# Prompt attention by pairs of heads, side by side on halves of TensorE's rows and columns

## The chip, the core and the metric

The kernel runs on one core of a Trainium2 chip. The core has TensorE (PE), VectorE (DVE), ScalarE (ACT), GpSimd (POOL) and SyncE (SP), each with its own instruction stream, kept in step by semaphores. Operands lie in SBUF; TensorE writes to PSUM, and VectorE, ScalarE or GpSimd carry results from there to SBUF. The metric is the device time in microseconds, lower is better.

## The reference

The program is one inference step of a decoder trunk of two layers, width 1024, for 256 new prompt tokens and 8 sequences of 8 sample tokens with 1024 past tokens each. A layer projects the tokens, mixes them by three head groups side by side (a Mamba-2 scan "SSD", causal pooling, and sparse attention "NSA"), adds an output projection, and ends with a convolutional feed-forward network. The change is in the prompt's part of the attention, which is, for four heads of width 64 and blocks of 128 queries:

```python
qb_len = min(Q_BLOCK, t)                                    # Q_BLOCK = 128, t = 256
def query_block(args):
    qb, gb, s = args
    sc = jnp.einsum('bqhd,bnd->bhqn', qb, ck)               # compressed keys
    pc = masked_softmax(sc, (cmp_end[None, :] <= tpos[:, None])[None, None])
    o_cmp = jnp.einsum('bhqn,bnd->bqhd', pc, cv)
...
    ss = jnp.einsum('bqhd,bqsd->bhqs', qb, kg)              # selected blocks
    ps = masked_softmax(ss, smask[:, None])
    o_slc = jnp.einsum('bhqs,bqsd->bqhd', ps, vg)
...
    sw = jnp.einsum('bqhd,bkd->bhqk', qb, kw)               # window
    pw = masked_softmax(sw, wmask[None, None])
    o_win = jnp.einsum('bhqk,bkd->bqhd', pw, vw)
    return gb[..., 0:1] * o_cmp + gb[..., 1:2] * o_slc + gb[..., 2:3] * o_win
```

All heads share one set of keys and values. With 256 prompt tokens there are four blocks of 64 to select from and 16 may be selected, so every block is taken.

## The kernel before

All 320 tokens (256 prompt, 64 sample) go through the dense products together. A dense product is a tile `mt` in PSUM: 128 outputs by 320 tokens, to which three products of split numbers are added (`xh` by `wh`, `xl` by `wh`, `xh` by `wl`). ScalarE makes the high part `wh` of a weight tile and VectorE the low part `wl`. Products of the attention are in plain fp32, and TensorE takes each of them in two passes.

A layer is cut into steps that a string names, one string for each layer. Those that matter here are `pr` (nsa_prep: turns queries and keys so that the head width of 64 lies on the partitions), `p0` and `p1` (prompt_scores for the first and second block of queries), `o0` and `o1` (prompt_out), `n0` and `n1` (new_rows: turned rows of the sample tokens in a tile `kn`), `s0` and `s1` (sample_scores of the two groups of four sequences), `l0` and `l1` (sample_load), `g` and `r0`, `r1` (gathers and the rest of the sample's attention), `st`, `c0` to `c3`, `x`, `z` (steps of the SSD). The numbers behind `@` are priorities. The tile framework's list scheduler puts the instructions of all steps in one order for each engine, by readiness and priority, and the pieces of `mt` are what it fills TensorE with. A table `ENG` says for some copies which engine makes them.

nsa_prep leaves the keys in `KT` (64 partitions: 256 keys of the selected kind, 16 compressed ones, 256 of the window) and the queries in `qT`, one slice of 64 partitions for each head. prompt_scores makes, for each head and key range (0 to 271, and for the second block also 272 to 527), one product `sc` into a PSUM tile, which VectorE or ScalarE carries to `Sx` (and VectorE the compressed keys' part to `Cx`); then maxima, exponentials, sums, and the weights scaled in place. prompt_out turns the compressed weights (`pct`) and, head by head, the others (`pT` in PSUM, `PT` in SBUF), and adds the products with the values to a tile `O` of two halves of 64 partitions, one for each head of a pair. Inside prompt_out, TensorE's instructions keep the order in which they are written. The PSUM pool `ns`, from which `sc`, `pT`, `O`, `kn`, `sC` and `sD` come, has three buffers.

SyncE issues the DMAs in its own order. A gather of cached rows (`cache<-cslc`) is 16 DMAs, each behind a load of a page number into a register. `wk` (line 1027) is the load of a sample group's window keys and values; `h<-s_ssm` loads the SSD states of the sample sequences.

## Time and profile before

| | before |
|---|---|
| median of 3 runs | 1232.06 us (1231.94 to 1237.4) |
| profiled execution | 1224.47 us |
| its span | 1222.3 us |
| granted TensorE clock, mean | 0.97 of full speed |
| busy: PE / DVE / ACT / POOL | 96% / 66% / 44% / 25% |
| DMA | 180.18 MB, 147 GB/s over the span |

The span is the time from the first to the last instruction of the one execution that the profiler recorded; that execution was 7.6 us faster than the median. A share of busy time is a mean over the whole span, so stretches are read apart from each other.

### The profile page before, as it was taken

How to read it: one execution, taken by the hardware profiler on the slowest of the kernel's cores; microseconds unless marked ns; L12 is line 12 of the kernel's file. 1: busy time of each engine (PE TensorE's matmuls, PEld its weight loads, DVE VectorE, ACT ScalarE, POOL GpSimd, SP SyncE). 2: the span in 40 equal slices, each digit the busy share in tenths (PEclk: the TensorE clock that was granted, in tenths of full speed). 3: DMA queues.
4: the chain of work that ended last, by engine and by line, in shares of the span. 5: the costliest groups of instructions: out<-in, count | busy, mean ns of one | idle time of the engine just before them, and what ended most of it. 6: DMA issues, size and time to landing. Idle time of an engine off the chain costs nothing.

```text
span 1222.3 us, 23199 instructions
## 1 busy us (share of the span) xinstructions
PE 1171.7 (96%) x8450; PEld 1093.2 (89%) x8450; DVE 802.5 (66%) x1661; ACT 536.7 (44%) x950; POOL 302.5 (25%) x616
## 2 busy tenths in 40 slices
PE   7999998899999999999999999889999999999995
PEld 6799765599999999999999877778899999999995
DVE  4583667368756666656663688986685666666665
ACT  5445523236454444433433565433455444444431
POOL 4732222100513113311300033440342311111111
PEclk9999999699999999999999999898899999999998
DMA  7634227355555455545433445206345544445421
GB/s 277 191 100 137 76 85 252 100 161 185 175 177 199 167 168 181 159 146 184 156 104 105 154 131 189 99 27 199 119 138 171 165 143 159 152 145 158 150 72 43
DMA packets 85186, 180.18 MB, mean 147 GB/s; under 512 B 10449, under 2 KB 45009, under 8 KB 84049
## 3 DMA queue, kind: packets, MB, share of 16 engines
q1 hardware_dynamic: 84048, 176.61, 45.0%
q0 software_dynamic: 1024, 2.10, 0.6%
q8 instruction: 66, 1.08, 0.4%
q14 instruction: 48, 0.39, 0.1%
HBM read 168.97 MB, written 13.83 MB: 150 GB/s over the span
## 4 chain that ended last, share of the span: by engine, by line
PE 88%; DVE 5%; POOL 2%; ACT 2%; issue 1%; DMA 1%; SPq 1%; DVEq 0%; POOLq 0%; ACTq 0%
PE mt L283 67%; PE cs L283 5%; PE nat L283 4%; PE sn L283 1%; PE O L283 1%; PE sb L283 1%; PE sc L283 1%; PE yoh L283 1%; PE ss L283 1%; PE pe L283 1%; PE rb L283 1%; PE pT L287 1%; DMA h<-s_ssm 1%; PE sA L283 1%; DVE xt L437 1%
## 5 line engine op out<-in xcount | busy, mean ns | idle before, releaser
L342 ACT ACTIVATE wh<-raw 128x1024 fp32r<-128x1024 f32 (+2 forms) x156 | 159.9, 1026 | 199.7 <-PE mt L283 147.2
L283 PE MATMUL mt<-xh,wa 128*128 128x320 f32 x1024 | 237.2, 310 | 0.0
L283 PE MATMUL mt<-xl,wh 128*128 128x320 f32 x736 | 232.0, 315 | 0.0
L283 PE MATMUL mt<-xh,wl 128*128 128x320 f32 x736 | 231.2, 314 | 0.0
L283 PE MATMUL mt<-xh,wh 128*128 128x320 f32 x736 | 230.9, 315 | 0.2 <-ACT xh L421 0.2
L290 DVE TENSOR_TENSOR wl<-raw,wh 128x1024 fp32r<-128x1024 f32 (+2 forms) x151 | 179.5, 1189 | 68.2 <-ACT wh L342 65.5
L283 PEld LDWEIGHTS mt<-xh,wa 128*128 128x128 f32 x1024 | 174.8, 188 | 0.3
L283 PE MATMUL mt<-xl,wa 128*128 128x320 f32 x512 | 158.5, 310 | 0.0
L283 PEld LDWEIGHTS mt<-xh,wh 128*128 128x128 f32 x736 | 138.9, 189 | 5.8 <-issue 5.0
L283 PEld LDWEIGHTS mt<-xh,wl 128*128 128x128 f32 x736 | 138.8, 189 | 4.6 <-issue 3.9
L283 PEld LDWEIGHTS mt<-xl,wh 128*128 128x128 f32 x736 | 139.0, 189 | 3.2 <-issue 2.4
L290 DVE TENSOR_TENSOR wa<-raw,wa 128x1024 fp32r<-128x1024 f32 x92 | 113.5, 1234 | 37.2 <-ACT wa L342 36.9
L290 POOL TENSOR_TENSOR fa<-fa,fc 128x256 f32<-128x256 f32 (+1 forms) x128 | 82.0, 662 | 191.5 <-ACT fc L1171 136.8
L342 ACT ACTIVATE wa<-raw 128x1024 fp32r<-128x1024 f32 x92 | 96.8, 1053 | 48.4 <-DMA raw<-wg 34.9
L283 PE MATMUL mt<-act,wa 128*128 128x320 f32 x768 | 117.8, 309 | 0.0
L283 PEld LDWEIGHTS mt<-act,wa 128*128 128x128 f32 x768 | 114.0, 188 | 0.0
L283 PE MATMUL mt<-act,wh 128*128 128x320 f32 x512 | 113.2, 309 | 0.0
L283 PEld LDWEIGHTS mt<-xl,wa 128*128 128x128 f32 x512 | 96.3, 188 | 0.0
L1164 POOL COPY off<-fext 128x2 f32<-128x2 f32 x64 | 19.5, 304 | 283.2 <-DVE fext L290 283.2
L283 PEld LDWEIGHTS mt<-act,wh 128*128 128x128 f32 x512 | 85.6, 188 | 0.0
L290 DVE TENSOR_TENSOR fo<-fo,mt 128x320 f32<-128x320 f32 x112 | 54.0, 484 | 44.6 <-PE mt L283 44.3
L283 PE MATMUL mt<-act,wl 128*128 128x320 f32 x256 | 79.1, 309 | 0.0
(375 smaller groups left out, 1976.2 us busy)
## 6 DMA issues: line engine op xcount, KB each, us to landing
raw<-wg SPq DMA_DIRECT2D x168, 512.0 KB
raw<-wd SPq DMA_DIRECT2D x64, 512.0 KB
cache<-cslc SPq DMA_DIRECT2D x128, 64.0 KB
cache<-ccmp SPq DMA_DIRECT2D x96, 64.0 KB
w<-w SPq DMA_DIRECT2D x4, 1024.0 KB
o_sss<-h SPq DMA_DIRECT2D x16, 256.0 KB
o_winold<-wnat SPq DMA_DIRECT2D x16, 252.0 KB
raw<-wnb SPq DMA_DIRECT2D x8, 384.0 KB
```

The costliest lines, as they stand in the source:

```text
L283: return PE.matmul(out, l, r, start=start, stop=stop, skip_group_check=True)
L287: return PE.transpose(out, in_, ident[:k, :k])
L290: return eng.tensor_tensor(out, a, b, op)
L342: ACT.activation(h, src, AF.Copy)
L437: DVE.scalar_tensor_tensor(t, mixo[k], w(k), rb if k else pb, op0=OP.mult, op1=OP.mult)
L1164: POOL.tensor_copy(off[:, m % 8, 0:2], ext[:, 256:258])
```

## The change

The keys stand twice in `KT`, on partitions 0 to 63 and 64 to 127, and the queries of two heads are turned at once, one head on each half of the partitions. prompt_scores takes two PSUM tiles for a pair of heads and issues the pair's two products one behind the other, the first on rows 0 to 63 of the array and the second on rows 64 to 127. prompt_out turns the heads 0, 1 and 2, then adds the first pair's products with the values, head 0 and 1 in turn (columns 0 to 63 and 64 to 127), then turns head 3, then adds the second pair's. The number of products with keys and values stays the same; there are four transposes of queries fewer in a layer, two more copies by VectorE (`ksd`) and one more product for the compressed keys (`ckp`).

```diff
-        c.KT = KT = s1.tile([64, 528], F32, name="KT", tag="KT")
-        c.qT = [n2([64, 4, 128], "qT") for _ in range(2)]
+        c.KT = KT = s1.tile([128, 528], F32, name="KT", tag="KT")
+        qT = n2([128, 2, 2, 128], "qT")
+        c.qT = [qT[:, 0], qT[:, 1]]
         kvd = n2([128, 2, 2, 2, 64], "kvd")
-        qd = n2([64, 4, 2, 64], "qd")
+        ksd = n2([128, 2, 2, 2, 64], "ksd")
         for u in range(2):
...
-            DVE.tensor_copy(qd[:, :, u], qn[2][:64].rearrange("p (h d) -> p h d", h=4))
+            DVE.tensor_copy(ksd[:, :, :, u], kvn[:, 0:2, 128:384].rearrange("p j (i d) -> p j i d", i=2)[:, :, :, 0:64])
...
-            transpose(ps[:64, 256:384], kvn[:, j, 128:192])
-            transpose(ps[:64, 384:512], kvn[:, j, 256:320])
+            for i in range(2):
+                transpose(ps[:, 256 + 128 * i:384 + 128 * i], ksd[:, j, i].rearrange("p u d -> p (u d)"))
...
-            for h in range(4):
-                transpose(ps[:64, 128 * h:128 * h + 128], qn[j][:, 64 * h:64 * h + 64])
-            cp(f"qT{l}{j}", "A", c.qT[j], ps[:64].rearrange("p (h t) -> p h t", h=4))
+            for m in range(2):
+                transpose(ps[:, 128 * m:128 * m + 128], qn[j][:, 128 * m:128 * m + 128])
+            cp(f"qT{l}{j}", "A", c.qT[j], ps[:, 0:256].rearrange("p (m t) -> p m t", m=2))
...
-        mm(ps[:64, 0:16], c.w2[:, 0:64], hc[:, 0, 0:16])
-        DVE.tensor_copy(KT[:, 256:272], ps[:64, 0:16])
+        for r in (0, 64):
+            mm(ps[r:r + 64, 0:16], c.w2[:, 0:64], hc[:, 0, 0:16])
+        DVE.tensor_copy(KT[:, 256:272], ps[:, 0:16])
...
-        for h in range(4):
-            lq = c.qT[qt][:, h]
-            for c0, cn in ((0, 272), (272, 256))[:nb]:
-                ps = nst("sc")
-                s0 = 256 if c0 else 0
-                mm(ps[:, :cn], lq, c.KT[:, c0:c0 + cn])
+        for m, (c0, cn) in [(m, k) for m in range(2) for k in ((0, 272), (272, 256))[:nb]]:
+            pss = [nst("sc") for _ in range(2)]
+            s0 = 256 if c0 else 0
+            for u in range(2):
+                r = slice(64 * u, 64 * u + 64)
+                mm(pss[u][:, :cn], c.qT[qt][r, m], c.KT[r, c0:c0 + cn])
+            for h, ps in enumerate(pss, 2 * m):
...
-            for h in range(4):
+            PT = {}
+
+            def turned(h):
                 ps = nst("pT")
...
-                PT = n2([128, 512], "PT")
-                cp(f"PT{c.l}{qt}{h}", "A" if h % 2 else "D", PT[:, :256 * nb], ps[:, :256 * nb])
-                r = 64 * (h % 2)
+                PT[h] = n2([128, 512], "PT")
+                cp(f"PT{c.l}{qt}{h}", "A" if h % 2 else "D", PT[h][:, :256 * nb], ps[:, :256 * nb])
+
+            def pair(m):
+
                 for i in range(2 * nb):
                     o = 192 if i % 2 == 0 else 320
-                    mm(pO[r:r + 64, 128 * (h // 2):128 * (h // 2) + 128], kvn[:, i // 2, o:o + 64],
-                       PT[:, 128 * i:128 * i + 128], start=False, stop=i == 2 * nb - 1)
+                    for h in (2 * m, 2 * m + 1):
+                        r = 64 * (h % 2)
+                        mm(pO[r:r + 64, 128 * m:128 * m + 128], kvn[:, i // 2, o:o + 64],
+                           PT[h][:, 128 * i:128 * i + 128], start=False, stop=i == 2 * nb - 1)
+            turned(0)
+            turned(1)
+            turned(2)
+            pair(0)
+            turned(3)
+            pair(1)
```

The scheduler's order moves with it. In layer 1, TensorE's row of the second block's scores (`p1`) stood like this before; the first four `sc` shown are head 1's second range, both of head 2, and head 3's first:

```order
L283 MATMUL sc_9303<-KT_8756,qT_8758 128x256
L283 MATMUL sc_9306<-KT_8756,qT_8758 128x272
L283 MATMUL sc_9310<-KT_8756,qT_8758 128x256
L283 MATMUL sc_9313<-KT_8756,qT_8758 128x272
L283 MATMUL mt_9471<-xh_8397,wh_9467 128x320
L283 MATMUL mt_9471<-xl_8398,wh_9467 128x320
L283 MATMUL mt_9471<-xh_8397,wl_9468 128x320
L283 MATMUL mt_9471<-xh_8397,wh_9467 128x320
L283 MATMUL sc_9317<-KT_8756,qT_8758 128x256
```

In the changed program the same place, with the end of `p0`, reads as follows; `sc_9242` and `sc_9243` are the second pair of `p0`, `sc_9290` and `sc_9291` the first pair of `p1`:

```order
L283 MATMUL sc_9242<-KT_8755,qT_8756 128x272
L283 MATMUL mt_9469<-xh_8396,wl_9466 128x320
L283 MATMUL sc_9243<-KT_8755,qT_8756 128x272
L283 MATMUL sc_9290<-KT_8755,qT_8756 128x272
L283 MATMUL sc_9291<-KT_8755,qT_8756 128x272
L283 MATMUL sc_9298<-KT_8755,qT_8756 128x256
L283 MATMUL mt_9469<-xh_8396,wh_9465 128x320
L283 MATMUL mt_9469<-xl_8397,wh_9465 128x320
```

Some pairs stand together and others have pieces of `mt` between their two products. In layer 0 all six pairs stand together.

In layer 0, TensorE's row of `o1`, from the first product with the compressed values on, was this:

```order
L283 MATMUL O<-pct,cvd 128x128 x2
L287 MATMUL pT<-cst,Sx 128x128 x4
L283 MATMUL cb<-BC 128x128 x2
L283 MATMUL mt<-xh,wl 128x320
L283 MATMUL mt<-xh,wh 128x320
L283 MATMUL mt<-xl,wh 128x320
L283 MATMUL mt<-xh,wl 128x320
L283 MATMUL mt<-xh,wh 128x320
L283 MATMUL O<-PT,kvn 64x128 x4
L287 MATMUL pT<-cst,Sx 128x128 x4
```

In the changed program it begins with the same product `O<-pct,cvd`, and the first products with the values stand behind the transposes of three heads:

```order
L283 MATMUL O<-pct,cvd 128x128 x2
L287 MATMUL pT<-cst,Sx 128x128 x8
L283 MATMUL mt<-xh,wl 128x320
L283 MATMUL mt<-xh,wh 128x320
L283 MATMUL mt<-xl,wh 128x320
L287 MATMUL pT<-cst,Sx 128x128 x4
L283 MATMUL O<-PT,kvn 64x128 x8
L287 MATMUL pT<-cst,Sx 128x128 x4
L283 MATMUL O<-PT,kvn 64x128
L283 MATMUL sC<-ckT,qsT 32x80 x4
L283 MATMUL sC<-wk,qsT 32x256
L283 MATMUL O<-PT,kvn 64x128 x7
```

Fewer pieces of `mt` stand between the steps of `o1`, and the first sample group's `sC` begins before the last values.

In layer 0, SyncE's row of the second group's sample gathers was this, where `cache_2430` and `cache_2591` are the two gathers of 16 DMAs and `wk_2426` is that group's window load:

```order
L460 TENSOR_LOAD pt_116
L460 ISA x2
L461 ISA
L461 DMA cache_2430<-cslc 128x128
L1027 DMA wk_2426<-wst 128x1024
L460 TENSOR_LOAD pt_116
L460 ISA x2
L461 ISA
L461 DMA cache_2591<-cslc 128x128
```

In the changed program the load of the window stands inside the first gather:

```order
L460 TENSOR_LOAD pt_116
L460 ISA x2
L461 ISA
L461 DMA cache_2429<-cslc 128x128
L1047 DMA wk_2425<-wst 128x1024
L460 TENSOR_LOAD pt_116
L460 ISA x2
L461 ISA
L461 DMA cache_2429<-cslc 128x128
```

Twelve of the sixteen DMAs of the first gather stand ahead of the window load and four behind it; all sixteen of the second gather follow. On VectorE, chunk 0's `cbm`, `xdt` and `G` of the SSD stood between the copies of `PT` of `o1`; they now stand behind the second sample group's `imp`. On TensorE, the chunk's state product `st` stood ahead of the second sample group's first `sA`; it now stands behind the third of its four.

## Rows read from the trace of the kernel before

**Rows 1.** The page's first part, and a group of its costliest

```profile
span 1222.3 us, 23199 instructions
...
PE 1171.7 (96%) x8450; PEld 1093.2 (89%) x8450; DVE 802.5 (66%) x1661; ACT 536.7 (44%) x950; POOL 302.5 (25%) x616
...
L283 PE MATMUL mt<-xh,wl 128*128 128x320 f32 x736 | 231.2, 314 | 0.0
```

**Rows 2.** The page's chain that ended last, by engine

```profile
PE 88%; DVE 5%; POOL 2%; ACT 2%; issue 1%; DMA 1%; SPq 1%; DVEq 0%; POOLq 0%; ACTq 0%
```

**Rows 3.** Stretches: us, then busy PE, PEld, DVE, ACT, POOL; PEclk, DMA, GB/s

```profile
145.00:165.00 20.00, 18.80 (x151) 15.51 (x149) 10.75 (x32) 9.00 (x27) 4.86 (x6) 1.00 0.17 50
...
290.00:630.00 340.00, 340.00 (x2316) 339.53 (x2314) 225.78 (x364) 150.63 (x208) 78.95 (x193) 1.00 0.52 167
700.00:730.00 30.00, 28.57 (x192) 22.00 (x191) 27.16 (x92) 20.40 (x68) 10.45 (x18) 1.00 0.37 109
```

**Rows 4.** Timeline of SyncE's queue, 140 to 180 us: start, us, line, operation

```profile
140.45 17.60 SPq L461 DMA_DIRECT2D cache<-cslc  x16
163.38 0.34 SPq L1027 DMA_DIRECT2D wk<-wst  x1
164.82 14.88 SPq L461 DMA_DIRECT2D cache<-cslc  x16
```

**Rows 5.** What SyncE's queue waited for, 120 to 240 us: total, times, longest

```profile
SPq L1027 <- PE sD L283: 5.2, 1, 5.2
```

**Rows 6.** TensorE's timeline, 165 to 183 us

```profile
170.31 1.13 PE L283 MATMUL st<-xde,bn 128*128 128x256 f32 x4
...
181.68 0.59 PE L283 MATMUL sA<-cache,qsT 64*32 64x512 f32 x1
```

**Rows 7.** The chain that ended last, 200 to 240 us: start, us, what

```profile
208.19 4.00 DMA h<-s_ssm
...
224.14 2.81 DMA h<-s_ssm
```

**Rows 8.** TensorE's timeline, 130 to 164 us: start, us, operation, passes (x)

```profile
134.52 1.15 PE L283 MATMUL sc<-KT,qT 64*128 64x272 f32 x4
...
149.78 0.33 PE L287 MATMUL pct<-cst,Pc 128*128 128x128 f32 x1 [0.90 <-POOL Pc L290]
...
151.97 0.71 PE L283 MATMUL O<-pct,cvd 128*128 128x128 f32 x4
...
160.28 0.66 PE L287 MATMUL pT<-cst,Sx 128*128 128x128 f32 x4
...
161.63 1.09 PE L283 MATMUL O<-PT,kvn 128*64 128x128 f32 x8
```

**Rows 9.** Tile sc by form: duration ns least/median/most, first and last start

```profile
L283 PE MATMUL sc<-KT,qT x48: 376/389/493, 102.0 to 706.7; 64*128 64x272 f32 x32, 64*128 64x256 f32 x16
L290 DVE TENSOR_TENSOR Sx<-sc,cst x16: 415/424/426, 102.8 to 707.1; 128x256 f32<-128x256 f32 x16
L290 DVE TENSOR_TENSOR Cx<-sc,cst x16: 114/164/175, 103.1 to 711.7; 128x16 f32<-128x16 f32 x16
L195 ACT ACTIVATE Sx<-sc x8: 357/383/386, 133.3 to 708.8; 128x256 f32<-128x256 f32 x8
```

**Rows 10.** TensorE's timeline: halves of columns, quarters of rows

```profile
177.69 1.09 PE L283 MATMUL abc<-cst,an 128*64 128x128 f32 x16
...
809.58 0.69 PE L283 MATMUL sn<-xde,bm 32*128 32x256 f32 x2
...
810.49 0.48 PE L283 MATMUL sn<-xde,bm 32*128 32x256 f32 x2 [0.22 <-DVE yof L290]
```

**Rows 11.** VectorE's timeline, 140 to 165 us

```profile
149.49 2.22 DVE L202 TENSOR_SCALAR Sx<-Sx,sx 128x256 f32<-128x256 f32 x8
```

**Rows 12.** What VectorE waited for, 684 to 770 us: total, times, longest

```profile
DVE Sx L290 <- PE sc L283: 2.4, 4, 0.7
...
DVE PT L196 <- PE pT L287: 0.7, 1, 0.7
```

More of the change, by code (lines that the diff above doesn't have):

```diff
@@ L896, in nsa_prep @@
                     cp(f"pv{l}{j}{i}{par}", "A" if par else "D", pv[r, i, :, 8 * j:8 * j + 8], v)
-            cp(f"KT{l}{j}", "A", KT[:, 272 * j:272 * j + 256], ps[:64, 256:512])
+            cp(f"KT{l}{j}", "A", KT[:, 272 * j:272 * j + 256], ps[:, 256:512])
             ps = nst("qT")
-            for h in range(4):
-                transpose(ps[:64, 128 * h:128 * h + 128], qn[j][:, 64 * h:64 * h + 64])
-            cp(f"qT{l}{j}", "A", c.qT[j], ps[:64].rearrange("p (h t) -> p h t", h=4))
+            for m in range(2):
+                transpose(ps[:, 128 * m:128 * m + 128], qn[j][:, 128 * m:128 * m + 128])
+            cp(f"qT{l}{j}", "A", c.qT[j], ps[:, 0:256].rearrange("p (m t) -> p m t", m=2))
         hc = n1("hc")[:, :64].rearrange("p (v k) -> p v k", v=2)
@@ L927, in nsa_prep @@
             DVE.tensor_copy(c.cvd[r, h], ps[r, 0:64])
+        qd = n2([64, 4, 2, 64], "qd")
+        for u in range(2):
+            DVE.tensor_copy(qd[:, :, u], qn[2][:64].rearrange("p (h d) -> p h d", h=4))
         c.qsT = s1.tile([128, 8, 4, 8], F32, name="qsT", tag="qsT")
@@ L957, in prompt_scores @@
         c.Sx.append(Sx)
-        for h in range(4):
-            lq = c.qT[qt][:, h]
-            for c0, cn in ((0, 272), (272, 256))[:nb]:
-                ps = nst("sc")
-                s0 = 256 if c0 else 0
-                mm(ps[:, :cn], lq, c.KT[:, c0:c0 + cn])
+        for m, (c0, cn) in [(m, k) for m in range(2) for k in ((0, 272), (272, 256))[:nb]]:
+            pss = [nst("sc") for _ in range(2)]
+            s0 = 256 if c0 else 0
+            for u in range(2):
+                r = slice(64 * u, 64 * u + 64)
+                mm(pss[u][:, :cn], c.qT[qt][r, m], c.KT[r, c0:c0 + cn])
+            for h, ps in enumerate(pss, 2 * m):
                 if nb == 1 or c0:
```

## The prediction

> **What bounds the kernel now.** I read the page's first lines before anything else: TensorE is busy 1171.7 of 1222.3 us [rows 1]. The reader should see how little is left over: 50.6 us, and whatever the change gives must come out of TensorE's own work or out of those microseconds. The chain that ended last says the same, 88% of it TensorE, with 1% each for DMA and for SyncE's queue [rows 2]. A share like that is an average over unlike stages, so I cut the span into stretches [rows 3]. In the feed-forward stretch from 290 to 630 us TensorE is busy 340.00 of 340.00 us; the change touches nothing there. In layer 0's prompt attention, 145 to 165 us, it is busy 18.80 of 20.00 and VectorE 10.75, so TensorE carries this stretch, much of it with pieces of the dense products (`mt`) put between the attention's steps. In layer 1's prompt attention, 700 to 730 us, VectorE is busy 27.16 of 30.00 us beside TensorE's 28.57: there two engines are close to full. Then I went to the queues, because an average hides what waits for a load. SyncE issues the gathers of the sample tokens' cached rows, one DMA after another: sixteen take 17.60 us from 140.45, then `wk` goes out at 163.38, then sixteen more take 14.88 us from 164.82 [rows 4]. Between them SyncE stands 5.2 us, until the last product `sD` of the first sample group gives back the buffer that `wk` needs [rows 5]. That wait is passed on: the last piece of `sA` starts at 181.68, two microseconds after the last gather went out at 179.70 [rows 6], and the state loads `h`, which stand behind the gathers on the same queue, are what the tail waits for (4.00 and 2.81 us on the chain [rows 7]).
>
> **The change, part by part.**
>
> *Scores.* Two heads' products (four passes) last 1.15 us in a row [rows 8]; a single pass lasts 0.389 us [rows 9], so three steps take 0.76 and one step 0.253 us. Issued on two halves of the rows, four passes take two steps: 0.51 us saved. There are 6 such pairs in a layer (2 for the first query block, 4 for the second), so 3.0 us. Do halves really run beside each other? The trace has products on quarters of the rows: `sn` alone takes 0.69 us for two passes, and in another place two passes are done in 0.48 us, hardly more than a single long pass [rows 10]. So yes, if nothing comes between them. In the order of layer 1 something does, `mt` or `kn`, in 4 of the 6 pairs; but there products of neighbouring pairs stand one behind the other on alternating halves, `sc_9243` to `sc_9298` and `sc_9299` to `sc_9312`, which makes four couples again, 2.0 us. Bounds: 0 and 3.0 us a layer.
>
> *Values.* Eight passes of `O` take 1.09 us [rows 8], 0.136 us each. Sixteen passes of `abc`, of the same size but alternating between halves of the columns, take the same 1.09 us [rows 10], 0.068 each. There are 48 passes in a layer (16 and 32): 48 x 0.068 = 3.3 us. Bounds: 0, if the wait for the tiles `PT` sets the pace and not the passes, and 3.3.
>
> *Transposes and copies.* Four transposes of queries fall away in a layer. Four transposes take 0.66 us [rows 8], the last one's end included, so 0.6 us. The second half of `ckp` adds two short passes, which I put at 0.1 us. The two copies into `ksd` replace nothing and cost VectorE some 0.4 us each by the copies of its score rows (0.424 us for 128x256 [rows 9]), 0.8 us a layer. They lie between the projections and the transposes, where TensorE has `mt` to do; if that cover were gone they would cost 0.8 us. The copies of KT and qT now cover twice the partitions with half or the same columns; I take that as no change, with 0.3 us either way as a bound.
>
> TensorE's own sum: layer 0 3.0 + 3.3 + 0.6 - 0.1 = 6.8, layer 1 2.0 + 3.8 = 5.8, together 12.6 us. This is the upper bound of the direct gain.
>
> *What of it reaches the end, layer 0.* The second block's steps run score, softmax, transpose, values, then the first sample group's `sC` and `sD`. In the order of before 16 pieces of `mt` stand between the first `O` and the first `sC`, and two more ahead of it; now 7 stand between `pct` and the last values, and the twelve transposes of three heads all come before the first values. What remains is 16 transposes (2.6 us), 32 passes of values (2.2), 7 pieces of `mt` of some 0.15 us (each 0.314 [rows 1], and one starts halfway through the other) and 0.5 for the first two `O`, 6.3 us, where it took 10.7 (151.97 to 161.63 + 1.09 [rows 8]). The softmax ahead of it, whose scaling of eight tiles starts at 149.49 [rows 11], begins when the last score is out, 3 to 4 us earlier (scores 1.0 + 2.0, the first block's values 1.1). So `sD`, now done just ahead of the 163.38 at which `wk` goes out, say at 163.2, is done some 8 us earlier, near 155. At SyncE `wk` now stands after the twelfth of the first sixteen gathers instead of after the sixteenth (the order shows it), which SyncE reaches at 140.45 + 12 x 1.1 = 153.6 [rows 4]. It waits some 1.4 us there, then runs on at its own pace, and its last gather goes out at 155 + 0.4 + 4 x 1.1 + 14.9 = 174.7 instead of 179.70. What stands behind the gathers comes earlier by that, **-5.0 us**; TensorE's own 6.8 us in this layer leaves room for it. Bounds: 0, if TensorE then waits elsewhere, and -6.8.
>
> *The SSD chunk.* VectorE's work for chunk 0 (`cbm`, `G`, `xdt`) moved from between the copies of `PT` to behind the second sample group's block selection, and `st` of chunk 0 now stands behind the third `sA` on TensorE. That piece needs the first eight of the last sixteen gathers, out at 174.7 - 7.4 = 167.3, and two microseconds until they land: 169.3, and `st` some 1 us later, 170.3, against 170.31 now [rows 6]. Nothing is lost, and nothing is to spare.
>
> *Layer 1.* There VectorE waits for TensorE's scores 2.4 us and for a transposed tile 0.7 us [rows 12] while being 91% busy. The most that faster products can give is those 3.1 us; between 0 and 3.1 I take **-2.0**, nearer to the upper end since TensorE itself has 5.8 us less to do there.
>
> Sum: 1222.3 - 5.0 - 2.0 = 1215.3 us of span. The profiled execution was 1224.47 us, 2.2 more than its span, so 1217.5; the median of the runs, 1232.06, lies 7.6 us above that execution, so the forecast is 1232.06 - 7.0 = **1225.1 us**. A change of 0.5% (6.2 us, a bound of 1225.9) is about what a measurement of this kernel can tell from none; 7.0 is just past it.
>
> **The rivals.**
>
> *Emptying of PSUM sets the pace.* A pair takes two of the three buffers at once, while `kn` holds the third for part of the time. Each buffer is emptied by 0.383 us of ScalarE or 0.424 of VectorE and 0.164 more for the compressed keys [rows 9]; a pair's products take 0.5 us, its emptying 0.8 to 1.05. The next pair would wait for that, and the 3.0 + 2.0 us of the scores are lost. For it: ten per cent of layer 1's VectorE is all that is free. Against it: `mt` pieces stand between the pairs in the new order and fill the time. Then `sD` comes some 7 us earlier rather than 8, the last gather 4.0 earlier, and layer 1, whose VectorE empties them, gives nothing: -4.0 us, **1228**. The Trainium skill, "TensorEngine Tiling (Array Packing)", section "PSUM Bottleneck", states this very thing: tiling speeds up TensorE and not the emptying of PSUM, and asks that both ScalarE and VectorE be used for it. By that page the scores would be worth nothing and the sum would be 1228; by the rows, in which `mt` covers the emptying, it is 1225.1.
>
> *The load stands too early (slower).* `wk` has moved ahead of four gathers. If `sD` is not at least 4 x 1.1 = 4.4 us earlier than 163.2, the four gathers behind `wk` are later than before, and all behind them. That is so if VectorE's and ScalarE's softmax, and not the scores, set the start of the transposes (in the rows `pct` starts at 149.78 after 0.90 us of waiting for GpSimd's `Pc` [rows 8]), and if the copies of `PT` hold up the transposes, all of which now come first. With `sD` where it is, the last gather is 4.4 us later, at 184.1, `sA` and the state loads with it, and layer 0 ends 4.4 us later: **1236.5**. It decides at a `sD` of 158.8.
>
> *The whole sum.* If TensorE is the bound in all of it, 12.6 us come back: **1219.5**. Against it speaks VectorE's 27.16 of 30 us in layer 1.
>
> That the halves don't overlap at all (1232) I count within the first rival; the rows of `abc` and `sn` speak against it.
>
> **How the numbers follow.** Forecast 0.48 (own range 1220 to 1229), whole sum 0.12, emptying 0.22, load too early 0.18. Faster by over 0.5%: 0.12 from the whole sum, 0.31 of the forecast's 0.48, 0.03 of the emptying's: 0.46. Slower by over 0.5% (above 1238.2): 0.13 out of the 0.18, since a later gather can also uncover a state load of 2.81 us. The rest, 0.41, within. The range reaches from the whole sum with another 4 us to the load too early: 1216 to 1238.
>
> **What would show it.** Right: in layer 0 the two `sc` of a pair start within some hundredths of a us; sixteen passes of `O` take about 1.0 us; SyncE issues `wk` after a wait of some 1.4 us rather than 5.2, and its last gather goes out near 175; the last `sA` is at 177 and `st` of chunk 0 no later than 170.5; the feed-forward stretches keep their 340 us. Wrong: a wait for a score buffer of over 2 us in a layer (emptying); `sD` after 158.8 and a wait at `wk` (load too early); the stretch from 700 us on in layer 1 as long as before (no -2.0 there). It would also be wrong if the tail's state loads come back with longer waits than the 4.00 and 2.81 us, since five microseconds won at the gathers would then be given back.

## The result, and the profile after

| | before | after |
|---|---|---|
| median | 1231.78 us (20 runs, 1222.45 to 1239.24) | 1238.09 us (20 runs, 1233.77 to 1242.52) |
| profiled execution; span | 1224.47; 1222.3 us | 1239.99; 1238.2 us |
| granted TensorE clock, mean | 0.970 | 0.958 |

The changed kernel takes 1.0068 times as long (95% interval 1.0047 to 1.0089): **slower by 0.7%**, where the forecast was faster by 0.6%. The two profiled executions lie 15.5 us apart and the medians 6.3 us: the one of before lay 7.3 us below its median, the one of after 1.9 us above. So a place in the trace is read below for what happens there, and only the timed runs say what it costs.

The page's first part after (answers to rows 1):

```profile
span 1238.2 us, 23202 instructions
...
PE 1185.1 (96%) x8446; PEld 1099.5 (89%) x8446; DVE 803.3 (65%) x1665; ACT 537.3 (43%) x950; POOL 298.8 (24%) x616
```

TensorE has four instructions fewer and is busy 13.4 us longer. The stretches of rows 3 after (us, then busy PE, PEld, DVE, ACT, POOL; PEclk, DMA, GB/s):

```profile
145.00:165.00 20.00, 17.16 (x113) 13.19 (x113) 9.98 (x32) 6.12 (x14) 1.11 (x3) 0.76 0.20 60
290.00:630.00 340.00, 340.00 (x2320) 337.97 (x2321) 227.49 (x363) 155.11 (x217) 81.06 (x195) 1.00 0.53 168
```

The feed-forward keeps its 340 us. Layer 0's prompt attention has two new things at once: TensorE is idle for 2.84 of 20 us in place of 1.20, and its mean granted clock is 0.76 in place of 1.00. I therefore cut layer 0 by events: from the first `O` to the first `gs`, on to the first `yoh`, and on to `pl`. Before:

```profile
125.40:167.80 42.40, 41.11 (x279) 31.66 (x277) 26.70 (x77) 18.61 (x51) 13.11 (x18) 1.00 0.26 76
167.80:190.10 22.30, 21.05 (x241) 14.89 (x237) 18.30 (x58) 8.58 (x20) 6.40 (x11) 1.00 0.53 173
190.10:231.50 41.40, 32.73 (x289) 18.95 (x278) 21.77 (x45) 8.39 (x19) 10.48 (x13) 0.75 0.53 176
```

After:

```profile
124.10:166.10 42.00, 34.42 (x217) 25.77 (x216) 22.68 (x68) 16.18 (x46) 5.92 (x11) 0.84 0.24 70
166.10:200.20 34.10, 33.85 (x304) 23.46 (x299) 25.27 (x70) 13.01 (x26) 10.98 (x17) 1.00 0.41 132
200.20:239.60 39.40, 33.38 (x273) 19.44 (x273) 18.96 (x40) 7.21 (x17) 10.94 (x13) 0.74 0.52 178
```

The first stretch is as long as before with 62 products fewer in it; these stand in the second, which is 11.8 us longer. From `O` to `pl` the layer takes 115.5 us in place of 106.1. Call length minus busy PE the idle time, and length times (1 - PEclk) the clock's loss: 7.6 us idle and 6.7 us of clock in the first stretch, against 1.3 and 0.

**The halves do run side by side, where nothing comes between them.** TensorE's timeline after, from the last pair of scores in layer 0 on:

```profile
133.56 0.73 PE L283 MATMUL sc<-KT,qT 64*128 64x256 f32 x4
...
140.42 0.27 PE L287 MATMUL kn<-cst,kvn 64*128 64x64 f32 x1 [3.01 <-DVE ckT L955]
142.42 0.63 PE L283 MATMUL mt<-xh,wl 128*128 128x320 f32 x1 [1.73 <-DVE wl L290]
142.86 0.47 PE L283 MATMUL mt<-xh,wh 128*128 128x320 f32 x1
143.12 0.47 PE L283 MATMUL mt<-xl,wh 128*128 128x320 f32 x1
...
150.16 0.33 PE L287 MATMUL pct<-cst,Pc 128*128 128x128 f32 x1 [1.90 <-POOL Pc L290]
...
160.00 1.09 PE L283 MATMUL O<-PT,kvn 128*64 128x128 f32 x14
```

The four passes of this pair take 0.73 us, where four passes took 1.15, and fourteen passes of values take the time of eight [rows 8]. Not every pair does as well: the six of layer 0 last 0.72, 1.54, 1.26, 1.00, 0.85 and 0.73 us, the longest with a wait for `Cx` inside, the next with a `kn` between its products. The last score is out at 134.3 us, 4.9 us earlier than in the trace of before (139.2). But `pct` starts at 150.16 and not at 149.78: the softmax between them has become 5.3 us longer. The rows show how. TensorE has nothing from 137.4 to 142.4 us but a `kn`; then `mt` pieces start every 0.27 us and not every 0.15, until 147.4, since the clock has fallen to the lower of its two levels (1.2 for 2.4 GHz) after that stretch with hardly any work. What it waited for is in VectorE's timeline, after:

```profile
137.44 1.23 DVE L629 SCALAR_TENSOR_TENSOR pld<-ua,cst,pex 64x64 f32<-64x64 f32 x1 [1.09 <-POOL ua L290]
...
141.15 1.22 DVE L290 TENSOR_TENSOR wl<-raw,wh 128x1024 fp32r<-128x1024 f32 x1
...
148.29 0.49 DVE L594 SCALAR_TENSOR_TENSOR sz<-mt,rb 128x320 f32<-128x320 f32 x1 [5.92 <-PE mt L283]
...
149.87 1.44 DVE L202 TENSOR_SCALAR Sx<-Sx,sx 128x256 f32<-128x256 f32 x5
```

The low part of the next weights, `wl`, stands on VectorE behind the pooling tiles `pld`, which wait for GpSimd. Counted by the pieces of `mt` that use it, the same `wl` was made 10.7 us earlier before, ahead of the pooling tiles of both halves, and TensorE came to it at 140.58 without a wait. VectorE's timeline before:

```profile
130.48 1.22 DVE L290 TENSOR_TENSOR wl<-raw,wh 128x1024 fp32r<-128x1024 f32 x1
131.61 0.47 DVE L628 SCALAR_TENSOR_TENSOR pld<-ua,cst,pex 64x256 f32<-64x256 f32 x1
```

So TensorE is ready for this `wl` some 3 us earlier than before, and VectorE makes it 10.7 us later. And `sz`, which waits 5.92 us for the slow `mt`, stands ahead of the softmax's sums, so the scaling of `Sx` starts at 149.87 (149.49 [rows 11]). The time that the scores gave stops here.

**The queue and the chunk.** SyncE's timeline, then what its queue waited for at `wk`, after (answers to rows 4 and 5):

```profile
141.37 12.58 SPq L461 DMA_DIRECT2D cache<-cslc  x12
161.79 0.34 SPq L1047 DMA_DIRECT2D wk<-wst  x1
162.90 18.12 SPq L461 DMA_DIRECT2D cache<-cslc  x20
```

```profile
SPq L1047 <- PE sD L283: 7.7, 1, 7.7
```

`sD` is done at about 161.7, not at 155: the wait has grown from 5.2 to 7.7 us, and the last gather goes out at 162.90 + 18.12 = 181.0 (179.70 [rows 4]). The second group's products and chunk 0's `st`, TensorE's timeline after (rows 6):

```profile
176.63 1.04 PE L283 MATMUL sA<-cache,qsT 64*32 64x512 f32 x2
177.60 0.33 PE L287 MATMUL xn<-cst,xsT 128*128 128x128 f32 x1
177.86 1.04 PE L283 MATMUL sA<-cache,qsT 64*32 64x512 f32 x2
...
183.97 1.13 PE L283 MATMUL st<-xde,bn 128*128 128x256 f32 x4
```

`st` is 13.7 us later (170.31 [rows 6]). And one product of `sA` (two passes) takes 1.04 us: these products use quarters of the columns and run beside each other when they stand together, but here a transpose stands between each two. The change put products side by side in one place and pulled such products apart in another.

**Layer 1** shows the same, in milder form. From the first `sc` to the first `pTs`, and on to the first `dec`, before:

```profile
696.40:733.40 37.00, 35.57 (x229) 27.16 (x229) 30.83 (x102) 21.46 (x69) 10.45 (x18) 1.00 0.41 129
733.40:774.50 41.10, 39.78 (x432) 33.49 (x429) 37.38 (x100) 22.83 (x49) 16.59 (x37) 1.00 0.54 186
```

After:

```profile
711.80:745.30 33.50, 32.16 (x224) 23.77 (x224) 30.61 (x102) 22.00 (x71) 10.40 (x16) 1.00 0.32 100
745.30:790.40 45.10, 42.85 (x435) 33.90 (x433) 37.54 (x101) 21.93 (x48) 16.54 (x37) 1.00 0.56 190
```

3.5 us are won and 4.0 given back. In the second stretch the sample tokens' products took, before (busy us, mean ns, idle):

```profile
L283 PE MATMUL sA<-cache,qsT 64*32 64x512 f32 x8 | 1.9, 590 | 0.0
L283 PE MATMUL sB<-cache,qsT 64*32 64x512 f32 x8 | 1.4, 601 | 0.0
L283 PE MATMUL sD<-wk,qsT 64*32 64x256 f32 x8 | 0.6, 388 | 0.0
L283 PE MATMUL sC<-wk,qsT 64*32 64x256 f32 x8 | 0.6, 376 | 0.0
```

and after:

```profile
L283 PE MATMUL sB<-cache,qsT 64*32 64x512 f32 x8 | 2.1, 601 | 0.1
L283 PE MATMUL sA<-cache,qsT 64*32 64x512 f32 x8 | 2.1, 601 | 0.0
L283 PE MATMUL sD<-wk,qsT 64*32 64x256 f32 x8 | 1.9, 388 | 0.0
L283 PE MATMUL sC<-wk,qsT 64*32 64x256 f32 x8 | 1.8, 385 | 0.0
```

A single product is as long as before. The four groups add up to 7.9 us and not 4.5 (6.4 and 3.4 if what runs at the same time is counted once), because pieces of `mt` and `O` now stand between them (there are 12 more pieces of `mt` in this stretch, which the first one no longer has).

### The profile page after: what moved, and what is told of

Its sections match the earlier page's. It is cut to its first block, busy times and chain, and to the rows that moved or that the text cites. A ratio compares the mean times of both kernels' runs of the same rounds, so it can differ in the third digit from the quotient of the medians.

```text
span 1238.2 us, 23202 instructions
## 1 busy us (share of the span) xinstructions
PE 1185.1 (96%) x8446; PEld 1099.5 (89%) x8446; DVE 803.3 (65%) x1665; ACT 537.3 (43%) x950; POOL 298.8 (24%) x616
## 4 chain that ended last, share of the span: by engine, by line
PE 89%; DVE 6%; POOL 1%; ACT 1%; issue 1%; DMA 1%; SPq 0%; DVEq 0%; POOLq 0%; ACTq 0%
PE mt L283 67%; PE cs L283 5%; PE nat L283 4%; PE sb L283 1%; PE sn L283 1%; PE dec L283 1%; PE sA L283 1%; PE ss L283 1%; PE O L283 1%; PE pe L283 1%; PE sc L283 1%; PE rb L283 1%; DMA h<-s_ssm 1%; PE Os L283 1%; DVE xt L437 1%
## 5 line engine op out<-in xcount | busy, mean ns | idle before, releaser
L290 DVE TENSOR_TENSOR wl<-raw,wh 128x1024 fp32r<-128x1024 f32 (+2 forms) x151 | 180.1, 1193 | 70.9 <-ACT wh L342 70.5
```

The costliest lines, as they stand in the source:

```text
L290: return eng.tensor_tensor(out, a, b, op)
```

## The experiments

Each ratio is to the kernel before on the same chip, with its 95% interval. On the chips of e5 to e16 the kernel before takes 1257.6 to 1263.2 us, and in every profile from them the stretch ahead of the first `sc` is some 30 us longer than the 100 to 104 us on the others; in e16 TensorE is busy 0.62 of the 20 us from 40 to 60, ahead of the first product that the change touches.

| kernel | ratio | `O` to `yoh` | `yoh` to `pl` | sample products, layers 0, 1 |
|---|---|---|---|---|
| before | 1 | 64.7 | 41.4 | 12.8, 9.6 |
| the change | 1.0068 [1.0047, 1.0089] | 76.1 | 39.4 | 16.7, 12.9 |
| e1 values only | 1.0061 [1.0022, 1.0101] | 70.0 | 38.4 | 16.7, 14.7 |
| e2 scores only | 0.9969 [0.9933, 1.0006] | 71.9 | 37.9 | 12.8, 11.1 |
| e12 scores only again | 0.9983 [0.9950, 1.0016] | 68.9 | 36.5 | 12.8, 11.1 |
| e9 the change again | 1.0034 [1.0005, 1.0063] | 75.2 | 39.2 | 16.7, 12.9 |
| e13 order only | 1.0127 [1.0083, 1.0172] | 70.5 | 38.4 | 16.1, 17.3 |
| e14 values only again | 1.0090 [1.0053, 1.0128] | 70.3 | 38.3 | 16.7, 14.8 |
| e15 two by two | 1.0004 [0.9969, 1.0039] | 69.3 | 37.4 | 13.4, 11.5 |
| e16 the change, third | 1.0061 [1.0037, 1.0085] | 75.2 | 39.2 | 16.7, 13.0 |
| e17 sample first | 1.0057 [1.0024, 1.0089] | 63.6 | 48.9 | 14.4, 10.5 |
| e18 sample first, two by two | 0.9963 [0.9931, 0.9995] | 61.3 | 41.8 | 12.7, 14.5 |

The stretches (us, of layer 0) and the busy time of `sA` to `sD` (us, of layer 0 from `O` to `yoh` and of layer 1 from `sc` to `dec`; each group by itself, so that groups which run at the same time count twice) are from one profile each, so a stretch shows where a kernel spends its time and is not to be set against a ratio to a few tenths of a per cent: the scores alone, too, move pieces of `mt` into `O` to `yoh` and are not slower for it.

Executions of one kernel differ mostly as their mean granted clock does: on the chip of e1 to e4 the kernel before took 1222.4 us at 0.973 and 1239.5 us at 0.958. Time multiplied by that clock is nearly the same in all executions of a kernel, so its mean gives an estimate of what a kernel would take against another at an equal clock. Means over the timed runs, before on the same chip, then the kernel:

| kernel | mean clock | time x clock, us |
|---|---|---|
| e9 the change again | 0.953, 0.953 | 1202.9, 1207.0 |
| e13 order only | 0.954, 0.947 | 1203.1, 1207.0 |
| e15 two by two | 0.954, 0.950 | 1203.1, 1198.1 |
| e16 the change, third | 0.954, 0.952 | 1203.1, 1206.3 |
| e17 sample first | 0.964, 0.954 | 1186.6, 1180.7 |
| e18 sample first, two by two | 0.964, 0.964 | 1186.6, 1183.0 |

The change loses 3 to 4 us that the clock does not explain (in e9 at an equal clock). By the same estimate e15 and e17 would be faster than before at an equal clock, by 5 and 6 us, and lose that to a lower one.

**Which part: e1, e2.** e1 takes the old nsa_prep and prompt_scores with the new prompt_out, e2 the reverse. For e1, for instance, a cut from its difference to the change:

```diff
-            for u in range(2):
-                r = slice(64 * u, 64 * u + 64)
-                mm(pss[u][:, :cn], c.qT[qt][r, m], c.KT[r, c0:c0 + cn])
+                mm(ps[:, :cn], lq, c.KT[:, c0:c0 + cn])
```

> Only prompt_out of the change (values by pairs); scores, keys and queries as before. Three theories of the loss. (A, order of the SSD) The new order of the values' products makes the scheduler put chunk 0 of layer 0's SSD behind the second sample group: in this kernel's order it stands there too, so it should be as slow as the whole change, 1235 to 1240 us, with the first `dec` after 170 us and the first `st` near 183. (B, softmax) VectorE's maximum of the scores stands behind a pooling tile, TensorE runs dry at 137 to 142 us and its clock falls: here the maximum stands ahead of the last pooling tiles, so TensorE should not run dry there, and the time should be 1229 to 1233. (C, scores) The pairs of scores crowd the PSUM buffers: absent here, so not slower than before, 1224 to 1231.

> Only the keys, queries and scores by pairs; prompt_out as before. (A, order of the SSD) chunk 0 stands where it stood before, ahead of pct, so not slower than before and up to 3 us faster: 1228 to 1232 us. (B, softmax) the maximum stands ahead of the last two pooling pieces, no dry stretch: the same. (C, scores crowd the PSUM buffers) as slow as the whole change: 1236 to 1240.

Measured 1.0061 and 0.9969. The loss comes with the values' part; the scores alone cost nothing, and may give a few tenths of a per cent. The products themselves are hardly the loss: in e1 the 48 passes of values in layer 0 keep TensorE busy for 4.4 us and not for 7.0.

**The maximum behind the pooling: e3.** VectorE's pooling `pld` of the second half in layer 0 is queued behind the softmax's maximum `nm`, by which that maximum no longer waits for GpSimd.

```diff
-                DVE.scalar_tensor_tensor(pld[r, 0:256], ...
+                with tc.issue_after(c.nmx.ins) if m and not l else nullcontext():
+                    DVE.scalar_tensor_tensor(pld[r, 0:256], ...
```

> The whole change, but in layer 0 the second half of the pooling tiles is queued on VectorE behind the scaling of the scores' maxima (nm); nothing else moves but one turn of kn on TensorE. (A, order of the SSD) little: 0 to -2 us against the change, 1236 to 1238, since 33 pieces of mt and the second sample group still stand ahead of chunk 0. (B, softmax) the exponentials start 2 us earlier, TensorE does not run dry at 137 to 142 us, its clock stays up: -4 to -6 us, 1232 to 1234. (D, the load stands too early, the prediction's rival) sD comes earlier and the wait at wk falls from 7.7 to about 3 us: -4, too, but with the gain seen at the last gather.

1.0047 [1.0017, 1.0076], with 7.2 us idle and 6.7 of clock as in the change: this theory fell. In its trace TensorE waits for `wl`, which still stands behind the pooling:

```profile
143.24 0.64 PE L283 MATMUL mt<-xh,wl 128*128 128x320 f32 x1 [4.35 <-DVE wl L290]
```

**The load too early: e4.** `wk` goes back behind the sixteenth gather in layer 0.

```diff
-            SP.dma_start(c.ws[g][kv], A["wst"][c.l, kv][:, 4 * g:4 * g + 4])
+            if g == 0 or c.l:
+                SP.dma_start(c.ws[g][kv], A["wst"][c.l, kv][:, 4 * g:4 * g + 4])
...
+        if g and not c.l:
+            for kv in range(2):
+                with tc.issue_after(pages[-1].ins):
+                    SP.dma_start(c.ws[g][kv], A["wst"][c.l, kv][:, 4 * g:4 * g + 4])
```

> The whole change, but the window load wk of the second sample group is queued behind the sixteenth gather, where it stood before; no other engine's order moves. (D, the load stands too early) SyncE's wait at wk falls from 7.7 to about 3 us and the last gather goes out near 177 instead of 181: -4 us, 1233 to 1235. (A and B) the gathers are not what TensorE waits for in the changed kernel, so the last gather comes earlier and the time stays: 1237 to 1239.

1.0045 [1.0011, 1.0078], and the stages of layer 0 within 0.2 us of the change's. The expectation had the wait at `wk` fall to about 3 us; it stayed at 7.6. The last gather goes out 56.4 us after the first `O` (56.9 in the change, 54.3 before), so four gathers more ahead of the load hardly bring it forward, and the load's place is not what makes the change slower. What a gather that does come earlier would give is not tested.

**The SSD earlier, the fours together, the pooling later: e5 to e8.** e5 gives the step `ss` priority (`ss@-60`), e7 queues chunk 0's transposes `xn` and `bn` behind the second group's `sB`, e6 queues the second half's pooling in layer 0 later, e8 does that with the scores' part alone.

```diff
-            for r, s in ((lo_, ua), (hi_, ub)):
+            with later(60 if m and not l else 0):
+              for r, s in ((lo_, ua), (hi_, ub)):
```

> The whole change, but layer 0's SSD has a priority 60 earlier: on every engine its order up to the first sample group is that of the change, and chunk 0's `dec`, `xn`, `bn` and `st` come ahead of the second sample group, whose four `sA` and four `sB` stand together again. The runs so far leave two theories. (A, order of the SSD) chunk 0 behind the second sample group is what costs: `st` comes near 175 instead of 184 us and the stretch from `gs` to the first `yoh` loses most of its 11.8 us more than before; the time falls by 5 to 8 us, to 1230 to 1233. (E, dry TensorE and clock) what costs is that TensorE runs dry at 137 to 152 us and gets the lower clock there: that stretch is unchanged here, so 1235 to 1238, whatever `st` does.

> The whole change, but in layer 0 the second half's pooling tiles `pld` on VectorE have a priority 60 later, so that a `wl` stands ahead of them and 58 pieces of mt can run ahead of `pct` instead of 42; the second sample group comes 23 pieces of mt earlier, chunk 0 of the SSD stays behind it. (E, dry TensorE and clock) no dry stretch at 137 to 152, clock 1.00 there: the stretch from the first `O` to the first `gs` loses 12 us of idle time and lower clock; the time falls by 6 to 10 us, to 1228 to 1232. (A, order of the SSD) chunk 0 is still behind the second sample group: no more than 2 us, 1236 to 1238.

> The whole change, but `xn` and `bn` of layer 0's chunk 0 are queued on TensorE behind the second sample group's `sB`, so that its `sA` and `sB` are not taken apart by them (they lasted 1.04 us each between the transposes, and four together take 0.6). (F, broken fours) the group's products take 1.9 us instead of 4.7: -3 us, 1235. Against it, chunk 0 comes later still: (A, order of the SSD) +3 us, 1241. (E, dry TensorE and clock) the stretch at 137 to 152 is unchanged, 1238.

> Scores, keys and queries by pairs, prompt_out as before, and the pooling tiles later as in the run before the last. A candidate for a version that beats both. Only-scores ran at 0.9969 of before; there the clock fell at 140 to 150 us for 3.3 us. (E, dry TensorE and clock) if the later pooling tiles keep TensorE fed there, 1223 to 1226; otherwise 1227.

1.0141 [1.0085, 1.0197], 1.0069 [1.0036, 1.0101], 1.0117 [1.0060, 1.0174] and 1.0061 [1.0030, 1.0093]. None is faster than before; each mends one place and loses elsewhere. The later pooling even takes the scores' part alone from 0.9969 and 0.9983 (e2, e12) to 1.0061 (e8). In e6 the dry stretch shrinks (4.9 us idle, 1.6 of clock), and `O` to `yoh` to 67.8 us, and its time is no better for it; e5 has its first `st` 49.6 us after the first `O` and not 59.9, but takes 50.5 us from `yoh` to `pl`, and e7 80.7 from `pl` to the feed-forward, where the change takes 39.4 and 70.5. (The 0.6 us in e7's expectation are four passes, which is two products; four products of `sB` last 1.07 us before, from 166.83 to 167.90.) The change was not run on that chip, so the next four repeat it.

**Repeats on one chip: e9 to e12.** e11 has, beside e6's edit, the transposes in another order, two blocks ahead of each pair:

```diff
             turned(0)
             turned(1)
-            turned(2)
             pair(0)
+            turned(2)
             turned(3)
```

> The changed kernel once more, as the measure for the three beside it: the last four ran where the kernel before took 1257.6 us and not 1231, with 30 us more ahead of layer 0's first score product, so they can't be set against the first four. If it is 1.005 to 1.009 of before here too, the loss does not hang on that; if it is larger, part of it lies in the start.

> The whole change with the second half's pooling tiles later, as before, now beside the change itself. In its profile the stretch from the first `O` to `pl` of layer 0 took 107.5 us against the change's 115.5. (E, dry TensorE and clock) so it should be 6 to 10 us faster than the change run beside it. (A, order of the SSD) at most 2 us faster.

> As the one before, and prompt_out turns heads 0 and 1, adds the first pair's values, turns heads 2 and 3, adds the second pair's. In its order the first four `dec` of chunk 0 stand ahead of `pct` again, as in the kernel before, and `st` ahead of the second group's `sA`. If both the dry stretch (E) and the SSD's place (A) cost, this is the best of all: faster than the kernel before by 3 to 8 us, 0.994 to 0.998. If only E costs, it is as the one before.

> Only keys, queries and scores by pairs, once more beside the change: 0.9969 of before in its first run. (A and E) it stands 8 to 12 us below the change here too; if it comes out at the change's time, its first result was the place and not the kernel.

1.0034 for the change, 1.0021 [0.9990, 1.0052] for the pooling later, 0.9988 [0.9951, 1.0025] for that with two by two, 0.9983 for the scores alone, which stand 3.5 us below the change and not 8 to 12. The pooling is at most a part. Two by two comes out lower than the pooling alone, but the intervals of the two overlap.

**Order or products: e13 to e16.** e13 keeps the scores of before and the new order of blocks, but issues each head's products one after another, so nothing of prompt attention runs side by side:

```diff
-                for i in range(2 * nb):
-                    o = 192 if i % 2 == 0 else 320
-                    for h in (2 * m, 2 * m + 1):
-                        r = 64 * (h % 2)
+                for h in (2 * m, 2 * m + 1):
+                    r = 64 * (h % 2)
+                    for i in range(2 * nb):
+                        o = 192 if i % 2 == 0 else 320
```

e14 repeats e1, e15 repeats e11, e16 is the change.

> Scores as before; the values' part in the changed order of blocks, but each head's products one after another. Theory (the order of layer 0's row costs, not the products): 1.004 to 1.008 of before, with TensorE idle for 6 to 8 us between the first O and the first gs, and the first st of layer 0 some 13 us later than before. Rival (the alternating products cost): 0.998 to 1.001.

> Scores as before, the values' part changed whole. Both theories: 1.004 to 1.008 of before, as in its first run (1.0061). The difference to e13 is the worth of the alternating alone: by the costing of the products 3 us a layer, 0.25% each, less than what reaches the end.

> The whole change, with the transposes two blocks and then their pair, and the pooling of the second half of layer 0 queued later; in layer 0 the decay products and the first chunk's products stand ahead of the sample groups, as before. Theory (order): 0.996 to 1.001 of before. Rival (products): 1.004 to 1.007, as the whole change beside it.

> The whole change, unchanged, as the control of this chip. Both theories: 1.003 to 1.009 of before; e15 is read against it.

1.0127, 1.0090, 1.0004, 1.0061. The order alone, with nothing side by side, costs as much as the change or more (1.004 to 1.008 was expected, and TensorE idles 3.6 us from `O` to `gs`, not 6 to 8), and the whole change in nearly the old order is not slower than before. So the products side by side are not what costs. The intervals of e13 and e14 overlap, so the worth of the alternating doesn't show; and e15 has the later pooling beside the other order. In e15 the pairs of heads and the sample tokens' products both stand together; TensorE's timeline there:

```profile
184.59 1.09 PE L283 MATMUL O<-PT,kvn 128*64 128x128 f32 x16
...
202.92 1.05 PE L283 MATMUL sA<-cache,qsT 64*32 64x512 f32 x4
```

Two products of `sA` in 1.05 us, where the change takes 1.04 for one. What e13 and e14 lose is not all in layer 0 (`O` to `pl` 2.8 and 2.6 us over before): sample products of 17.3 us in layer 1 in e13 against 9.6, and in e14 a stretch of layer 1 at the lower clock (below).

**Giving the sample tokens' products priority: e17, e18.** In the order of instructions these products stand in 12 unbroken runs before, 22 in the change, 25 in e13 and 13 in e15. e17 is the whole change with

```diff
+        with later(-2000):
             for b in B:
                 mm(pC[o[b], 256:336], qsT[64 * g:64 * g + 64, 4 * g + b], c.ckT[g][:, b])
```

around `sC`, `sD`, `sA` and `sB`; e18 has the two by two order as well. Neither has the later pooling.

> The whole change; only the sample tokens' products sC, sD, sA and sB have priority over what else is ready, so that they stand in 15 runs in place of 22, and in layer 0 the decay products and the first chunk's state product stand ahead of the second sample group again. Theory (these products pulled apart, with the chunk's place, are what costs): 0.994 to 1.000 of before, the sample products back from 16.7 and 12.9 us to about 13 and 11. Rival (the dry stretch ahead of pct and its clock alone): that stretch is not addressed, 1.004 to 1.007 as in the change.

> As the kernel before it, with two blocks of transposes ahead of each pair in place of three and one; the sample products stand in 12 runs, as before. Theory: 0.992 to 0.999 of before, the gain of the side by side products at last kept. Rival: 1.003 to 1.007.

The same three stretches of layer 0, e17:

```profile
129.30:163.80 34.50, 32.78 (x244) 23.92 (x242) 23.74 (x70) 16.68 (x48) 9.76 (x16) 1.00 0.27 82
163.80:193.00 29.20, 26.42 (x257) 17.75 (x255) 22.39 (x65) 11.55 (x24) 7.71 (x11) 0.88 0.46 151
193.00:241.90 48.90, 42.24 (x287) 23.94 (x276) 19.73 (x41) 7.15 (x17) 10.47 (x14) 0.62 0.42 143
```

and e18:

```profile
127.40:161.70 34.30, 32.17 (x246) 24.10 (x244) 23.08 (x69) 16.82 (x48) 9.71 (x16) 1.00 0.28 84
161.70:188.70 27.00, 24.93 (x256) 17.52 (x252) 22.56 (x65) 10.81 (x23) 6.41 (x12) 1.00 0.49 158
188.70:230.60 41.90, 33.98 (x273) 19.57 (x273) 20.43 (x42) 7.55 (x19) 9.06 (x13) 0.74 0.50 168
```

The priority alone brings back the old place of the chunk and of the decay products, and the dry stretch is gone in both (PEclk 1.00). e18 is faster than before, 0.9963 [0.9931, 0.9995] (1225.97 us, 12 runs, against 1232.47), the only kernel here whose whole interval is. It differs from e17 by the order of the transposes alone, on one chip, and the two intervals lie apart: this is the clearest pair of runs for an order that changes the time. Where the gain over before lies, its profile doesn't show: of the 2.9 us less from `O` to `pl` (103.2 against 106.1), 2.3 us stand more ahead of the first `O` (25.7 us from the first `sc`, where before takes 23.4), and in layer 1 some of its sample products run at the lower clock (gs to dec loses 3.4 us to it). No run gives the kernel before the same priority, so how much of the gain is the change's and how much the priority's is not shown.

e17 has won 12.5 us against the change from `O` to `yoh`, and gives them back: 2.8 us ahead of the first `O`, and 48.9 us from `yoh` to `pl` at a mean clock of 0.62, where the change takes 39.4 at 0.74; 1.0057 in the end. So the theory that I wrote ahead of e17 fell as far as it made the broken runs and the chunk's place the whole of the cost. The rival's number came out, but not its mechanism, since its dry stretch is gone. What e17 loses it loses to the clock: 0.954 against e18's 0.964 in the timed runs, and at an equal clock, by the estimate above, it would be the faster of the two. So between these two the order of the transposes shows only through the clock; why e17's clock stays low is open.

## Why the prediction was wrong

- **The step that failed** is the one headed "What of it reaches the end, layer 0". It let the softmax begin with the last score and let everything behind it move up, to a `sD` "near 155". The last score did come 4.9 us earlier, more than the 3 to 4 put there, but the `wl` that TensorE needs next was made 10.7 us later, behind pooling tiles that wait for GpSimd, and the sums of the softmax stand behind a `sz` that waits for those `mt` pieces. `sD` came 1.6 us earlier and the -5.0 us became 0: the last gather is 1.3 us later than before. Then the same step counted the pieces of `mt` that no longer stand between the parts of `o1` as gone from the path; they stand behind the first sample group, and the stretch to `yoh` is 11.8 us longer.
- **The same step took an order for a wait.** It read the last `sA`, which starts two microseconds after the last gather, as held up by it, and the state loads of the tail as held up by the gathers ahead of them. In the trace of before TensorE waits for no gather between 160 and 235 us. All its waits there are these:

```profile
PE yoh L283 <- DMA h<-s_ssm: 6.7, 2, 5.2
PE sn L283 <- ACT bm L201: 1.1, 2, 0.9
PE imp L283 <- DVE imp L1055: 0.9, 2, 0.7
PE yd L283 <- DVE G L290: 0.9, 1, 0.9
PE st L283 <- POOL xde L290: 0.4, 1, 0.4
```

  And the state load of 4.00 us at 208.19 [rows 7] follows VectorE's `h`, which ends at 207.73 on the same chain, 28 us after the last gather. So even five microseconds won at the queue had nothing here that waited for them.
- **"Nothing is lost, and nothing is to spare"** at the SSD chunk: `st` came 13.7 us later. The step took the gathers as what `st` waits for; it stands behind the moved `mt`, the decay products and `sA`.
- **The terms of TensorE's own sum** were right in kind and too large. In busy time the values' 48 passes fell from 7.0 to 4.8 us in either layer (2.2 of the 3.3 forecast, in layer 0 partly at the lower clock), the scores from 6.8 to 5.7 us in layer 0 (1.1 of 3.0) and from 7.2 to 6.0 in layer 1 (1.2 of 2.0). What has no term at all is the sample tokens' products, which were side by side before: +3.9 and +3.3 us, group by group. That cancels **layer 1's -2.0**: it was won (3.5 us up to `pTs`) and lost.
- **Emptying of PSUM** did not set the pace: in the trace the products of scores wait 0.2 us for one in either layer. The Trainium skill, "TensorEngine Tiling (Array Packing)", section "PSUM Bottleneck", warns of it; no run here shows it, with three buffers and `mt` pieces between the pairs.
- **The load stands too early** came out near the measured time (1236.5 against 1238.1) and its condition was met (`sD` at 161.7, after 158.8), but with the load back in its place (e4) the time and the stages of layer 0 stay. A rival that gives the right number is not yet the right mechanism.
- **What is shown and what not.** Shown: the order that came with the values' part costs, by itself (e13 against before) and in the change (e18 against e17, one edit apart; e15, which also has the later pooling, against e16); and 3 to 4 us of the loss are there at an equal clock (e9, e16). Read from traces, not separated by a run: how much of it is the dry stretch, and how much the sample products and the chunk behind them; e15, e17 and e18 change them together. That the order moves the clock as well is seen in e13 and e17 (between e17 and e18 it is the whole difference), and why it does is open.

## What to carry to other kernels

A faster stage in a list-scheduled program moves everything that was tuned around it: before counting a gain, list what else TensorE has in that stretch, what feeds it, and which products already run side by side and could be pulled apart. Where TensorE carries a stretch, ask whether the engines that make its next operand keep up once it is faster; if they don't, the saving becomes idle time, and the clock can take more behind it. If a variant of the order costs more than the change itself gives, try the change in two or three orders before judging it: here 1.0068 and 0.9963 are the same products, the second in another order and with the sample tokens' products first.

## What the runs showed of the hardware that I had not expected

- A stretch of 5 us with hardly any TensorE work is followed by 5 us in which `mt` pieces start every 0.27 us and not every 0.15, and the 2 us without work ahead of `pct` by another such stretch: 7.6 us idle from `O` to `gs` brought 6.7 us of clock with them.
- How soon the clock comes back varies from profile to profile. After `pl`, with TensorE busy for 4.00 of each 4 us, the mean granted clock was 0.64 in the first 4 us and 1.00 in the next before; in the change's profile it was 0.50, 0.50 and 0.69 in the first three. The stretch from `pl` to the feed-forward is 3.7 us longer for it. A second such place is the stretch ahead of layer 1's first turned keys: 31.3 us at 0.95 before, 34.7 us at 0.83 after. Together these are 7.1 of the 15.9 us between the two spans, and nothing in the change is near either; in another profile of the change (e16) the first of them is as before (67.5 us at 0.98), the second is not.
- The clock also fell where TensorE had been busy throughout. In e14, layer 1:

```profile
735.00:740.00 5.00, 5.00 (x21) 3.04 (x20) 2.44 (x12) 1.44 (x2) 0.00 (x0) 0.78 0.49 156
740.00:750.00 10.00, 10.00 (x25) 6.83 (x26) 5.05 (x22) 4.76 (x19) 0.00 (x0) 0.50 0.07 21
```

  The profile of e1, the same kernel on another chip, loses the same 11.8 us to the clock in that stage. Both profiled executions are slower than their kernel's median (1280.37 against 1270.54 us, 1245.01 against 1238.54), so this does not happen in every execution. No run here says why.
